# A two-layer decoder trunk on one core: the engines' order in the middle passes of the MLPs is written out slot by slot

## The chip, the cores and the metric

The kernel runs on one core of one Trainium2 chip. The time is the device time of one execution in microseconds (us). The engines of the core are called as the profile calls them: PE (TensorE, matrix products), PEld (its weight loads), DVE (VectorE), ACT (ScalarE), POOL (GpSimd) and SP (SyncE, which issues the loads here). Each engine works through its own list of instructions from front to back and waits where an input is not there yet.

## The reference: what is computed

Two layers over 256 positions with a width of 2048. The first layer mixes with a gated short convolution, the second with latent attention; behind each mixer stands the same MLP, with a hidden width of 8192:

```python
def sq_relu_mlp(x, w1, w2):
    return jnp.square(jax.nn.relu(x @ w1)) @ w2

h = layer_norm(ALPHA * h + mix, ...)
h = layer_norm(ALPHA * h + sq_relu_mlp(h, mlp_w1[layer], mlp_w2[layer]), ...)
```

All inputs and outputs are float32. The change lies in the two MLPs.

## The kernel before: tiles, stages and order

**Precision.** A float32 operand is split into two parts, hi and lo: hi is a rounding cast on ACT (`split`, line 139) and lo the remainder on DVE (line 140). A product is made of the large parts and the two mixed terms. Every weight that is loaded (tiles `raw`, 128x1024, 512 KB, from a pool of 7) passes through such a cast and such a subtraction into a pair hi, lo (a pool of 9).

**The MLP in passes.** The hidden width is cut into 8 passes q of 8 blocks m of 128 columns. For one block, `mm_run` (16 pairs of matmuls, lines 227 and 231) makes `x @ w1` into a PSUM bank called "unit". `whole` then empties the bank: ACT copies its right half (line 370), DVE adds it to the left half into a row tile `fp` or `fq` (line 371). Only when that is done may the next `mm_run` write the bank. Relu and square follow on ACT (line 768), or for the last block on DVE (line 764).

**The middle passes, 1 to 6, and the first half of pass 7 in the second MLP** multiply with `w2` by Strassen's scheme: seven products in place of eight. For this, `form` (lines 655 to 666) makes sums of two neighbouring blocks on DVE, `finish_pair` splits the row into `factors` (tiles h1a, h1c, h3a, h3c; a cast of 128x896 on ACT and a subtraction on DVE), and the weights are combined too. A weight item is a pair of loads r1, r2. `prepare` makes of it t = b12 - r1 (line 174), two half-wide sums (lines 178 and 181), and the splits of r1, t, r2 and of a half-wide tile t4. The tile t is a `raw` too.

**Slots.** `steps` yields the slots (q, m). A slot holds the `mm_run` of block (q, m) and, where there is one, one product item: `fast_products`, 21 matmuls (lines 312 to 314) into seven PSUM banks. The product items run `SHIFT` = 6 blocks behind: slots 0 to 5 of pass 1 have none, nor in the first MLP the last two of pass 7. A slot without a product is called lone here. In the second MLP two products stand alone behind pass 7. The weights stand in `stream` in the order of the slots: two w1 halves (singles), then the w2 pair.

**Two column halves.** Products 0 to 3 of a pass belong to one half of the output columns, 4 to 7 to the other. When product 3 has ended, the seven sums are moved out of PSUM (`put_back`, line 624, ACT) and those of the other half moved in (`resume`, line 718, ACT). In the text one such pair of copies is a move. Behind the last middle pass, `fold` (line 632) adds up the sums on DVE, eight additions for a half, drawn by `next(folds)`.

**What sets the order before.** The matmuls of `mm_run` and `fast_products` are pinned to program order. DVE's and ACT's instructions are not: a scheduler orders them by program order as priority and by when their inputs are due. The weights are made ahead by `take`: a look ahead of 6 or 7 steps, where a single is one step and a pair three. The seven moves stand together in the program, behind the product that ends a half. The row of block 2 is a tile of its own, `fq`, since two rows are open there; all other rows share one `fp`. In the second MLP `issue_after` holds back what follows the last `finish_pair`.

Of the kernel before, what the change touches and what calls it, by code (L numbers as in the profile page):

```python
# [10 lines left out]
F32 = mybir.dt.float32  # L11
F32R = mybir.dt.float32r
AF = mybir.ActivationFunctionType
ALU = mybir.AluOpType
# [23 lines left out]
SHIFT = 6  # L38
# [18 lines left out]
def trunk(ctx: ExitStack, tc: tile.TileContext, xT, vecs, lead, w_first, w_in, w_out, w_kv, w_q, w_uk, w_uv,  # L57
# [95 lines left out]
    def prepare(i):  # L153

        if len(stream[i]) == 1:
            raw = load_raw(i, stream[i][0])
# [13 lines left out]
        finished(r1, f"{i}_1")  # L170
        yield
        t = raws.tile([P, 1024], F32, tag="raw", name=f"raw{i}_t")
        two = "p (a c) -> p a c"
        nc.vector.tensor_tensor(t.rearrange(two, a=2), b12.unsqueeze(1).to_broadcast([P, 2, BW]),  # L174
                                r1.rearrange(two, a=2), ALU.subtract)
        finished(t, f"{i}_t")
        yield
        nc.vector.tensor_tensor(b12, b22, t[:, :BW], ALU.subtract)  # L178
        finished(r2, f"{i}_2")
        t4 = r1[:, :BW]  # L180
        nc.vector.tensor_tensor(t4, b21, b12, ALU.subtract)  # L181
# [7 lines left out]
    def size(i):  # L189

        return 1 if len(stream[i]) == 1 else 3

    begun = {}
# [31 lines left out]
    def high(ps, w, blk, x, first):  # L225

        return nc.tensor.matmul(ps, w[blk // 8][0][:, blk % 8, :], x, start=first, stop=False)  # L227

    def low(ps, w, blk, x, last):

        return nc.tensor.matmul(ps[:, :T], w[blk // 8][1][:, blk % 8, :], x[:, :T], start=False, stop=last)  # L231

    def mm_run(wps, x, k0, k1, nk, turned=None, pin=lambda ins: ins):

        for k, (w, ps) in [(k, u) for k in range(k0, k1) for u in wps]:
            if k == turned:
                pin(low(ps, w, k, x[k], False))
            pin(high(ps, w, k, x[k], k == 0))
            if k != turned:
                pin(low(ps, w, k, x[k], k == nk - 1))  # L240
# [68 lines left out]
    def dot(ps, w, x, first, last, onto=False, pin=lambda ins: ins):  # L309


        pin(nc.tensor.matmul(ps, x[0], w[0], start=first, stop=False, skip_group_check=onto))  # L312
        pin(nc.tensor.matmul(ps, x[0], w[1], start=False, stop=False, skip_group_check=onto))  # L313
        pin(nc.tensor.matmul(ps, x[1], w[0], start=False, stop=last, skip_group_check=onto))  # L314
# [45 lines left out]
    def fast_products(ps, x, j, fresh, ready, onto=()):  # L360

        b, = take(1, 6)
        a = {n: [x[j // 2][:, j % 2, o, i * P:(i + 1) * P] for o in range(2)] for i, n in enumerate(LEFT, 1)}
        for p, l, r in FACTORS:
            dot(ps[p], b[r], a[l], p in fresh, p in ready, onto=p in onto, pin=tc.keep_in_program_order)
# [224 lines left out]
    def mlp(idx, ln, blocks, fast, begin=None, extra=None, last=False):  # L590
# [64 lines left out]
        def form(u, v):  # L655

            a21, a11, a22, a12, s1, s3, s2, s4 = ((u if i < 4 else v)[:, i * P:(i + 1) * P] for i in range(8))
            nc.vector.tensor_tensor(s1, a21, a22, ALU.add)
            if u is v:
                two = u.rearrange("p (i c) -> p i c", c=P)  # L660
                nc.vector.tensor_tensor(two[:, 5:7, :], two[:, 0:5:4, :], a11.unsqueeze(1).to_broadcast([P, 2, P]),
                                        ALU.subtract)
            else:
                nc.vector.tensor_tensor(s2, s1, a11, ALU.subtract)
                nc.vector.tensor_tensor(s3, a21, a11, ALU.subtract)
            nc.vector.tensor_tensor(s4, a12, s2, ALU.subtract)

        def finish_pair(j, u):
            f = factors[j // 2][:, j % 2]
            if q in FAST or last:  # L670
                v = row() if u.shape[1] < 8 * P else u
                form(u, v)
                at = P if q in FAST else 0
                if u is not v:
                    split(f[:, 0, at:4 * P], f[:, 1, at:4 * P], u[:, at:])
                    at = 4 * P
                return split(f[:, 0, at:], f[:, 1, at:], v[:, at:])
            return split(f[:, 0, :2 * T], f[:, 1, :2 * T], u[:, :2 * T])

        def row():  # L680
            return fast.tile([P, 8 * P], F32, tag="fp", name="fp")
# [29 lines left out]
        def resume(p, g, at=None):  # L711
# [3 lines left out]
            if p in OWN and begun[g] == FAST[0]:  # L715
# [5 lines left out]
        begun = {0: FAST[0], 1: FAST[0]}  # L721
        rows = {}
        behind = ExitStack()

        def products_of(p, i, j, g):
# [3 lines left out]
            end = i == 0 or p == FAST[-1] and not last  # L729
            fast_products(ps, factors, j, set(fresh), order if j == NB - 1 and end else (), onto)  # L730
            fresh.clear()
            if j == NB - 1 and end:
                begun[g] = 0
                for o in order:
                    if p == NQ - 1:
                        if o in OWN:
                            put_back(o, g, ps[o])
                        continue
                    put_back(o, g, ps[o])
                    if i == 0:  # L740
                        resume(o, 1 - g)
            if p == FAST[-1] and j == NB - 1 and end:
                folds = chain(folds, fold(g))

        for q, m, pair in steps(last):
            lone = pair is None
            if q == NQ:
                products_of(*pair)
                if pair[2] == NB - 1:
                    behind.close()  # L750
                continue
            if q == FAST[0] and m == SHIFT:
                for o, _, _ in FACTORS:
                    resume(o, 1)
            w = take(2, 7)
            at = "6" if lone and (m - SHIFT) % 2 else "unit"
            un = psum("ps_u", bank[at])
            mm_run([(w, un)], xhl, 0, NC, NC, turned=TURNED if TURN(q, m) else None, pin=tc.keep_in_program_order)
            if m % 2 == 0:
                u = act.tile([P, 2 * T], F32, tag="ab", name="fq") if m == 2 and not lone else row()  # L760
            whole(un, u[:, (m % 2) * T:(m % 2 + 1) * T])
            late = m >= QC - 2
            if late and m % 2:
                nc.vector.scalar_tensor_tensor(u[:, T:2 * T], u[:, T:2 * T], 0.0, u[:, T:2 * T], ALU.max, ALU.mult)
            elif late or m % 2:
                for function in (AF.Relu, AF.Square):
                    at = u[:, :T] if late else u[:, :2 * T]
                    nc.scalar.activation(at, at, function)
            if late and q not in FAST and not last:
                f, at = factors[m // 4][:, 1], slice(m % 2 * T, (m % 2 + 1) * T)  # L770
                split(f[:, 0, at], f[:, 1, at], u[:, at])
            else:
                rows[m // 2] = u
            if m % 2 and (m > 3 or lone) and m // 2 in rows:
                made = finish_pair(m // 2, rows.pop(m // 2))
                if last and q == NQ - 1 and m == QC - 1:
# [454 lines left out]
```

## Time and profile before

| | |
|---|---|
| median of 3 runs | 2020.77 us (2018.97 to 2022.5) |
| the profiled execution | 2020.92 us |
| its span | 2019.1 us |
| middle passes, first MLP | 452 to 1008 us of the span |
| middle passes, second MLP | 1405 to 1983 us of the span |

A row of the timeline gives the start in the span, the duration, the engine, the line of the kernel, the operation, the tiles (out<-in), and in square brackets how long the engine had stood idle before it and for whom. Durations of neighbours overlap a little, so what one instruction costs its engine in a busy stretch is the distance between two starts. A row of the waits gives who waited for whom, with the total, the number of times and the longest. A row of the windows gives for a stretch of time the busy time of each engine with the number of instructions, then PE's granted clock (1.00 is full speed), the share of the DMA engines and GB/s.

### The profile page before, as it was taken

Reading aid. Unit: us, or ns where it says so; the run is one execution under the profiler, and the core shown is the slowest. Engines: PE = TensorE matmul, PEld = TensorE weight load, DVE = VectorE, ACT = ScalarE, POOL = GpSimd, SP = SyncE. Lnnn points to the kernel's source line nnn. Section 1 sums busy time; section 2 is a strip of 40 time slices with the busy share of each in tenths; the row PEclk is TensorE's granted clock in tenths of the full one; section 3 lists DMA queues with packets and bytes.
Section 4 is the critical chain, followed back from the end, with each engine's and each line's share of the span. In section 5 each row is a group of like instructions: output and inputs, shape, how many; then the busy total and the mean of one; then the engine's idle time right before and its main releaser. Section 6 shows DMA issues by size and latency. Waiting matters only on the chain.

```text
span 2019.1 us, 29666 instructions
## 1 busy us (share of the span) xinstructions
PE 1990.8 (99%) x11050; PEld 1731.3 (86%) x11050; DVE 1747.1 (87%) x2562; ACT 1289.2 (64%) x1927; POOL 5.6 (0%) x27
## 2 busy tenths in 40 slices
PE   9999999999999999999999999999999999999998
PEld 8888888988888888888889998898888888888885
DVE  8667677778899999999998988777889999999998
ACT  6444445586667767677756665557666776767763
POOL 0000000000000000000000000000000000000000
PEclk9999999999999999999999999999999999999999
DMA  9666666575556555666665544556455556555554
GB/s 343 213 188 188 188 189 189 186 234 153 174 200 202 198 201 187 207 206 201 235 223 160 180 132 140 183 191 185 147 187 208 188 189 208 200 205 190 198 176 158
DMA packets 107712, 390.00 MB, mean 193 GB/s; under 512 B 11952, under 2 KB 12720, under 8 KB 107056
## 3 DMA queue, kind: packets, MB, share of 16 engines
q1 hardware_dynamic: 106560, 383.79, 57.6%
q0 software_dynamic: 864, 4.19, 0.5%
q8 instruction: 86, 1.41, 0.3%
q14 instruction: 58, 0.48, 0.1%
q10 hardware_dynamic: 144, 0.13, 0.0%
HBM read 383.87 MB, written 4.19 MB: 192 GB/s over the span
## 4 chain that ended last, share of the span: by engine, by line
PE 80%; DVE 10%; ACT 6%; issue 3%; DMA 1%; DVEq 0%; ACTq 0%
PE ps_u L227 15%; PE ps_l L227 13%; PE ps_u L231 8%; PE ps_l L231 7%; PE ps L313 5%; PE ps L314 5%; PE ps L312 4%; DVE lo L140 4%; PE ps_d L313 2%; PE ps_d L314 2%; PE ps_d L312 2%; ACT hi L139 2%; ACT ps L718 2%; PE ps_w L261 2%; PE ps_w L260 2%
## 5 line engine op out<-in xcount | busy, mean ns | idle before, releaser
L140 DVE TENSOR_TENSOR lo<-raw,hi 128x1024 fp32r<-128x1024 f32 x710 | 856.2, 1220 | 163.8 <-ACT hi L139 94.7
L139 ACT CAST hi<-raw 128x1024 fp32r<-128x1024 f32 x710 | 732.2, 1055 | 201.8 <-PE ps_l L227 102.2
L227 PE MATMUL ps_u<-xhl,hi 128*128 128x512 f32 x1792 | 624.4, 395 | 17.3 <-DVE fq L371 12.9
L231 PE MATMUL ps_u<-xhl,lo 128*128 128x256 f32 x1792 | 486.2, 280 | 0.0
L227 PEld LDWEIGHTS ps_u<-xhl,hi 128*128 128x128 f32 x1792 | 329.8, 188 | 90.2 <-DVE fq L371 17.2
L231 PEld LDWEIGHTS ps_u<-xhl,lo 128*128 128x128 f32 x1792 | 338.9, 189 | 12.2
L227 PE MATMUL ps_l<-xhl_a,hi 128*128 128x512 f32 x704 | 244.1, 393 | 0.0
L231 PE MATMUL ps_l<-xhl_a,lo 128*128 128x256 f32 x704 | 195.4, 279 | 0.0
L139 ACT CAST hi_t<-raw_t 128x1024 fp32r<-128x1024 f32 x100 | 105.9, 1059 | 118.3 <-DVE raw_t L174 111.2
L227 PEld LDWEIGHTS ps_l<-xhl_a,hi 128*128 128x128 f32 x704 | 132.1, 188 | 29.9
L370 ACT COPY t<-ps_u 128x256 f32<-128x256 f32 x112 | 41.9, 374 | 151.0 <-PE ps_u L231 151.0
L231 PEld LDWEIGHTS ps_l<-xhl_a,lo 128*128 128x128 f32 x704 | 131.9, 188 | 0.2
L174 DVE TENSOR_TENSOR raw_t<-raw,raw 128x1024 f32<-128x1024 f32 x100 | 121.9, 1219 | 6.6 <-DMA raw<-in_w2f_dram 6.6
L140 DVE TENSOR_TENSOR lo_t<-raw_t,hi_t 128x1024 fp32r<-128x1024 f32 x100 | 121.9, 1219 | 2.3 <-ACT hi_t L139 2.3
L227 PE MATMUL ps_l<-z,hi 128*128 128x512 f32 x240 | 82.4, 391 | 0.0
L261 PE MATMUL ps_w<-xd,hi 128*128 128x258 f32 x256 | 72.7, 284 | 0.0
L259 PE MATMUL ps_w<-xd,hi 128*128 128x258 f32 x256 | 72.3, 282 | 0.0
L260 PE MATMUL ps_w<-xd,lo 128*128 128x258 f32 x256 | 72.2, 282 | 0.0
L139 ACT CAST t<-raw 128x512 fp32r<-128x512 f32 x100 | 61.9, 619 | 15.4 <-DVE raw L181 15.2
L227 PE MATMUL ps_l<-oT,hi 128*128 128x512 f32 x208 | 71.3, 391 | 0.0
L181 DVE TENSOR_TENSOR raw<-raw 128x512 f32<-128x512 f32 x100 | 69.0, 690 | 2.3
L178 DVE TENSOR_TENSOR raw<-raw,raw_t 128x512 f32<-128x512 f32 x100 | 68.5, 685 | 1.0
(371 smaller groups left out, 3897.3 us busy)
## 6 DMA issues: line engine op xcount, KB each, us to landing
raw<-in_w_dram SPq DMA_DIRECT2D x312, 512.0 KB, 4.2
raw<-in_w2f_dram SPq DMA_DIRECT2D x200, 512.0 KB, 5.1
raw<-in_w_in_dram SPq DMA_DIRECT2D x88, 512.0 KB, 3.7
raw<-in_w_out_dram SPq DMA_DIRECT2D x32, 512.0 KB, 3.7
raw<-in_w_o_dram SPq DMA_DIRECT2D x32, 512.0 KB, 4.2
raw<-in_w_kv_dram SPq DMA_DIRECT2D x10, 512.0 KB, 4.5
raw<-in_w_q_dram SPq DMA_DIRECT2D x8, 512.0 KB, 3.9
raw<-in_w_uk_dram SPq DMA_DIRECT2D x8, 512.0 KB, 4.4
```

The costliest lines, as they stand in the source:

```text
L139: nc.scalar.copy(hi, src)
L140: return nc.vector.tensor_tensor(lo, src, hi.bitcast(F32), ALU.subtract)
L174: nc.vector.tensor_tensor(t.rearrange(two, a=2), b12.unsqueeze(1).to_broadcast([P, 2, BW]), r1.rearrange(two, a=2), ALU.subtract)
L181: nc.vector.tensor_tensor(t4, b21, b12, ALU.subtract)
L227: return nc.tensor.matmul(ps, w[blk // 8][0][:, blk % 8, :], x, start=first, stop=False)
L231: return nc.tensor.matmul(ps[:, :T], w[blk // 8][1][:, blk % 8, :], x[:, :T], start=False, stop=last)
L259: nc.tensor.matmul(ps[:, :W], hi, x[k][:, :W], start=k == 0, stop=False)
L260: nc.tensor.matmul(ps[:, :W], lo, x[k][:, :W], start=False, stop=False)
L261: nc.tensor.matmul(ps[:, :W], hi, x[k][:, W:], start=False, stop=k == NC - 1)
L312: pin(nc.tensor.matmul(ps, x[0], w[0], start=first, stop=False, skip_group_check=onto))
L313: pin(nc.tensor.matmul(ps, x[0], w[1], start=False, stop=False, skip_group_check=onto))
L314: pin(nc.tensor.matmul(ps, x[1], w[0], start=False, stop=last, skip_group_check=onto))
```

## The change

The lists of PE, DVE and ACT in the middle passes become the program's own order: a class `Order` links each instruction of these three engines to the one before it on the same engine. SP is not linked. `SHIFT` becomes 5: the lone slots are slots 0 to 4 of pass 1 and, in the first MLP, the last three of pass 7; one product stands alone at the end of the second MLP. What a slot needs is made wholly in the slot in front of it. `prepare` has five steps for a pair in place of three, and they are laid between the slot's other work; the moves are taken one at a time from a list and laid between the splits. A slot that begins with open moves is called crowded in the code. With `SHIFT` 5 only one row is open at a time, so `fq` goes, and each row is formed and split in one piece. The number of matmuls is the same. The remaining edits (`pin`, `two`, names) only follow from this.

```diff
-SHIFT = 6
+SHIFT = 5
...
     def prepare(i):
...
+            raw = loaded.pop(i) if i in loaded else load_raw(i, stream[i][0])
...
         r1, r2 = (load_raw(f"{i}_{j}", src) for j, src in enumerate(stream[i]))
+        t = raws.tile([P, 1024], F32, tag="raw", name=f"raw{i}_t")
...
-        finished(r1, f"{i}_1")
-        yield
...
         nc.vector.tensor_tensor(t.rearrange(two, a=2), b12.unsqueeze(1).to_broadcast([P, 2, BW]),
                                 r1.rearrange(two, a=2), ALU.subtract)
+        yield
+        finished(r1, f"{i}_1")
+        yield
+        nc.vector.tensor_tensor(b12, b22, t[:, :BW], ALU.subtract)
+        t4 = r1[:, :BW]
+        nc.vector.tensor_tensor(t4, b21, b12, ALU.subtract)
         finished(t, f"{i}_t")
         yield
-        nc.vector.tensor_tensor(b12, b22, t[:, :BW], ALU.subtract)
         finished(r2, f"{i}_2")
-        t4 = r1[:, :BW]
-        nc.vector.tensor_tensor(t4, b21, b12, ALU.subtract)
+        yield
         f = state["fast"].tile([P, 2, BW], F32R, tag="t4", name=f"t4_{i}", bufs=2)
         split(f[:, 0, :], f[:, 1, :], t4)
...
+    class Order:
+        def __init__(self):
+            self.at, self.last = len(tc.nc.cur_bb.bb.instructions), {}
+        def keep(self):
+            traced = tc.nc.cur_bb.bb.instructions
+            for i in traced[self.at:]:
+                if i.engine in ENGINES:
+                    if i.engine in self.last:
+                        tc.add_manual_dep(i, self.last[i.engine], mybir.DependencyInfo(
+                            mybir.DependencyClass.NoSync, mybir.DependencyReason.DATA), reason="order")
+                    self.last[i.engine] = i.name
+            self.at = len(traced)
...
+        def move(n):
+            for _ in range(n):
+                if moves:
+                    o, g, on = moves.pop(0)
+                    put_back(o, g, ps[o])
+                    if on:
+                        resume(o, 1 - g)
...
+        order = Order()
+        for s, (q, m, pair, own) in enumerate(slots):
             lone = pair is None
...
+            following = slots[s + 1][3] if s + 1 < len(slots) else []
+            pairs = [i for i in following if size(i) > 1]
+            ahead = [i for i in range(state["next"], (following or own)[-1] + 1) if i not in own and i not in begun]
+            if not pairs:
+                ahead = [i for i in range(state["next"], own[-1] + 6) if i not in own and i not in begun]
+                ahead = ahead[:next((k for k, i in enumerate(ahead) if size(i) > 1), len(ahead))]
+            singles = [i for i in ahead if size(i) == 1]
+            for i in singles:
+                loaded[i] = load_raw(i, stream[i][0])
...
+            if q < NQ:
+                w = take(2, 0)
+                at = "6" if lone and (m - SHIFT) % 2 else "unit"
+                un = psum("ps_u", bank[at])
+                mm_run([(w, un)], xhl, 0, NC, NC, turned=TURNED if TURN(q, m) else None)
...
+            crowded = len(moves) > 0
+            for i in pairs:
+                step(i)
+            for i in singles:
+                step(i)
+                move(1)
+            if crowded:
+                evacuate()
+            for i in pairs:
+                step(i)
+            move(len(moves))
+            for i in pairs:
+                step(i)
+            if rows and m == 2:
+                finish_pair(0, rows.pop(0))
             if pair:
                 products_of(*pair)
-            if m in (2, 3) and not lone:
-                finish_pair(m - 2, rows.pop(m - 2))
+            if not crowded:
+                evacuate()
+            if q < NQ and m == QC - 1:
+                forms(rows[m // 2])
+            move(1)
+            for i in pairs:
+                step(i)
+            move(1)
+            if q < NQ and m == QC - 1:
+                finish_pair(m // 2, rows.pop(m // 2))
+            for i in pairs:
+                step(i)
+            move(2)
+            if q < NQ:
+                if m % 2 or m == QC - 2:
+                    u = rows.get(m // 2)
+                    if m < QC - 1:
+                        at = u[:, :T] if m == QC - 2 else u[:, :2 * T]
+                        for function in (AF.Relu, AF.Square):
+                            nc.scalar.activation(at, at, function)
+                        if m % 2:
+                            forms(u)
+                            if m > 1 or lone:
+                                finish_pair(m // 2, rows.pop(m // 2))
...
+                if q == NQ - 1 and m:
+                    for _ in range(3 if m >= SHIFT else 2):
+                        next(folds, None)
+            order.keep()
+        move(len(moves))
```

Here `evacuate` is `whole` (with line 764 for block 7), and `step(i)` makes the next step of item i.

More of the change, by code (lines that the diff above doesn't have):

```diff
@@ L742, in products_of @@
-            if p == FAST[-1] and j == NB - 1 and end:
-                folds = chain(folds, fold(g))
-        for q, m, pair in steps(last):
-            lone = pair is None
[L747 to L751, printed above, removed]
+            if end:
+                opened[g] = 0
+                moves.extend((o, g, i == 0 and p < NQ - 1) for o in order if p < NQ - 1 or o in OWN)
+                if p == FAST[-1]:
+                    folds = chain(folds, fold(g))
@@ L752, in mlp @@
             if q == FAST[0] and m == SHIFT:
+                sums = act.tile([P, 4, 2, BW], F32, tag="xres", name=f"sums{idx}")
                 for o, _, _ in FACTORS:
                     resume(o, 1)
[L755 to L773, printed above, removed]
```

120 lines of the change are left out of this document (54 added, 66 removed).

## The prediction

> **What bounds the kernel now.** I read the busy shares first, then what PE waited for, then one steady pass of the middle passes in the windows and what DVE waited for in it (the last two rows), then the timeline around PE's wait.
>
> ```profile
> span 2019.1 us, 29666 instructions
> PE 1990.8 (99%) x11050; PEld 1731.3 (86%) x11050; DVE 1747.1 (87%) x2562; ACT 1289.2 (64%) x1927; POOL 5.6 (0%) x27
> ...
> PE ps_u L227 <- DVE fq L371: 12.9, 10, 1.8
> PE ps_u L227 <- DVE fp L371: 4.4, 4, 1.6
> PE ps L313 <- DVE lo_t L140: 1.0, 1, 1.0
> PE ps L312 <- ACT hi_t L139: 0.6, 1, 0.6
> ...
> 709.70:794.27 84.57, 83.21 (x425) 70.59 (x425) 80.12 (x100) 60.16 (x84) 0.00 (x0) 1.00 0.60 199
> ...
> DVE lo L140 <- ACT hi L139: 3.6, 2, 3.4
> DVE fp L371 <- ACT t L370: 0.5, 1, 0.5
> ```
>
> PE is the busiest, and nothing here makes its work smaller: the most that an order can win is its waits. But the steady pass is not PE's. DVE is busy 80.12 of its 84.57 us and waits 4.1 for ACT (the last two rows); the 0.35 left are small gaps. So DVE closes the loop, and PE waits once a pass, for the bank that DVE empties late. The reason stands in the timeline:
>
> ```profile
> 697.88 0.58 ACT L624 COPY acc<-ps 128x512 f32<-128x512 f32 x1
> 698.35 0.59 ACT L624 COPY sums<-ps 128x512 f32<-128x512 f32 x1
> 698.83 0.60 ACT L718 COPY ps<-acc 128x512 f32<-128x512 f32 x1
> 699.35 0.60 ACT L718 COPY ps<-sums 128x512 f32<-128x512 f32 x1
> ...
> 705.28 0.64 ACT L718 COPY ps<-acc 128x512 f32<-128x512 f32 x1
> ...
> 705.47 1.23 DVE L140 TENSOR_TENSOR lo<-raw,hi 128x1024 fp32r<-128x1024 f32 x1 [3.70 <-ACT hi L139]
> ...
> 709.70 0.50 PE L227 MATMUL ps_u<-xhl,hi 128*128 128x512 f32 x1 [1.37 <-DVE fq L371]
> ```
>
> ACT makes the seven moves nearly in one go, from 697.88 to 705.9; no cast comes out, DVE stands still for 3.70, and 4 us later PE waits 1.37 for DVE. A move costs ACT 0.47 + 0.52 = 1.0 by the starts.
>
> **The lengths.** What an instruction costs a busy engine is the distance of two starts:
>
> ```profile
> 680.50 2.35 DVE L140 TENSOR_TENSOR lo<-raw,hi 128x1024 fp32r<-128x1024 f32 x2
> 682.77 1.22 DVE L174 TENSOR_TENSOR raw_t<-raw,raw 128x1024 f32<-128x1024 f32 x1
> 683.91 0.42 DVE L371 TENSOR_TENSOR fp<-ps_u,t 128x256 f32<-128x256 f32 x1
> 684.24 0.68 DVE L178 TENSOR_TENSOR raw<-raw,raw_t 128x512 f32<-128x512 f32 x1
> 684.96 0.69 DVE L181 TENSOR_TENSOR raw<-raw 128x512 f32<-128x512 f32 x1
> 685.57 1.22 DVE L140 TENSOR_TENSOR lo_t<-raw_t,hi_t 128x1024 fp32r<-128x1024 f32 x1
> ...
> 1971.38 0.29 DVE L658 TENSOR_TENSOR fp<-fp 128x128 f32<-128x128 f32 x1
> 1971.70 0.42 DVE L661 TENSOR_TENSOR fp<-fp 128x256 f32<-128x256 f32 x1
> 1972.16 0.29 DVE L666 TENSOR_TENSOR fp<-fp 128x128 f32<-128x128 f32 x1
> 1973.57 1.23 DVE L140 TENSOR_TENSOR h3a<-fp,h3a 128x1024 fp32r<-128x1024 f32 x1 [1.12 <-ACT h3a L139]
> ...
> 651.53 0.39 PE L312 MATMUL ps<-hi,h1a 128*128 128x512 f32 x1
> ...
> 656.34 0.39 PE L227 MATMUL ps_u<-xhl,hi 128*128 128x512 f32 x1
> ...
> 661.90 0.39 PE L312 MATMUL ps<-hi,h1c 128*128 128x512 f32 x1
> ```
>
> A full-wide DVE instruction costs 1.135, emptying the bank 0.33 (its end 0.42 behind its start), the half-wide ones 0.72 (the next one needs it) and 0.61; t4's split, half-wide too, 0.60. Two groups of ACT in the steady pass and one of the whole run give the casts of a row, relu and square, and the copy of the bank:
>
> ```profile
> L139 ACT CAST h1a<-fp 128x896 fp32r<-128x896 f32 x2 | 1.9, 947 | 0.0
> L768 ACT ACTIVATE fp<-fp 128x512 f32<-128x512 f32 x4 | 2.5, 628 | 0.0
> ...
> L370 ACT COPY t<-ps_u 128x256 f32<-128x256 f32 x112 | 41.9, 374 | 151.0 <-PE ps_u L231 151.0
> ```
>
> On PE a product takes 4.81 (651.53 to 656.34) and an `mm_run` 5.56, so a slot 10.37 and eight 82.96.
>
> **The change, on DVE.** Per slot six full-wide instructions, t4's sums and split and the emptying: 6.81 + 0.72 + 0.61 + 0.60 + 0.33 = 9.07, before as after. The order decides what else is lost. Before the emptying now stand t, both singles, r1, the half-wide sums and the split of t: 7.0 us, then 0.42. If DVE begins a slot's list by a lag L behind PE, PE waits as soon as L + 7.42 exceeds 10.37, that is at L over 2.95. The slots then differ:
> - Blocks 4, 6 and 0: only the 9.07. L falls by 1.30.
> - Blocks 3 and 5: the forms stand together, so each waits for the one before (0.32 + 0.46); then ACT must cast the row before DVE may subtract, and nothing stands between. The last rows above show just this: 1.41 from the last form to the subtraction; the cast of 128x896 is some 0.10 shorter than that of 128x1024, so 1.31; the subtraction 1.00 (1.09 less the overlap). Together 3.09; L grows by 1.79. Now other splits lie in these gaps.
> - Block 7: line 764, 0.45, forms 0.98, and the subtraction 1.00 (r2's split covers the cast): L grows by 1.13.
> - Block 1: forms 0.98, and the moves. Four of them lie in slot 0, behind the product; with r2's cast, which waits for DVE's sum, ACT is through about 2.0 us into slot 1. DVE comes at lag 1.4 and then waits: for the first single 0.6, for the second behind a move 0.8, for ACT's copy of the bank 0.1, for r1's cast 0.6. That is 2.1, where the bunch cost 4.1. L grows by 1.78.
> - Block 2: row 0 is subtracted ahead of the emptying, 1.00: L falls by 0.30, but 8.0 + 0.42 stand before the bank is free.
>
> The sum of a pass is 8 x 9.07 + 2 x 3.09 + 2.43 + 3.08 + 1.0 = **85.25 us, against 84.57 now**: the bunch's wait is halved, but waits for the row's cast (2.2 in blocks 3 and 5) and in the forms come instead. PE has to wait 85.25 - 82.96 = 2.3 a pass. In place: L is 3.2 behind block 1, so block 2's bank is free at 3.2 + 8.42 = 11.6, 1.3 late; behind blocks 3 and 5 L is about 3.4, and blocks 4 and 6 are 0.4 late each; 0.1 is lost at each restart.
>
> **Where passes begin.** In a lone slot DVE has little to do, but its list waits for PE, and behind the bank of block 3 stands a chain: ACT's copy 0.37, DVE's add 0.42, relu and square of 0.63 each, forms 1.1, cast 0.95, subtraction 1.0, some 5.4 with the hand-overs. Only then begin the parts of the first pair, 6.8 us of DVE in a slot of 5.56 of PE. L comes to 6.7 in slot 5, whose bank is free at 6.7 + 7.42 = 14.1: 3.7 late, and 1.7 more in the next, 5.5 in all. From below: the start now loses 1.6 in one wait at a bank (the longest of the four fp waits). I take the middle, 3.5.
>
> **Where they end.** Eight `fold` additions of 0.60 lie in blocks 1 to 4 of pass 7, 4.8 us. In the first MLP the last three slots are lone and swallow most of it: 2.8 of waits. In the second DVE's surplus of that pass is 2.3 + 4.8; PE waits 6.9.
>
> ```profile
> L632 DVE TENSOR_TENSOR acc<-acc,sums x18: 678/686/694, 956.2 to 1938.5; 128x512 f32<-128x512 f32 x18
> ...
> 963.83 0.50 PE L227 MATMUL ps_u<-xhl,hi 128*128 128x512 f32 x1 [1.81 <-DVE fq L371]
> ...
> 965.00:970.50 5.50, 5.50 (x24) 4.76 (x23) 5.50 (x7) 1.65 (x3) 0.00 (x0) 0.69 0.52 187
> ...
> 1918.10 0.50 PE L227 MATMUL ps_u<-xhl,hi 128*128 128x512 f32 x1 [1.81 <-DVE fq L371]
> ...
> 1922.00:1926.00 4.00, 4.00 (x22) 3.41 (x21) 4.00 (x5) 0.37 (x1) 0.00 (x0) 1.00 0.76 278
> ...
> 1978.00:1984.00 6.00, 5.42 (x17) 4.33 (x18) 6.00 (x7) 5.79 (x9) 0.00 (x0) 0.72 0.73 188
> ```
>
> **The clock.** Behind the wait of 1.81 at 963.83 PE ran below full clock: a mean of 0.69 over 5.5 us, 1.7 us lost. Behind the same wait at 1918.10 it did not. Behind the two waits of the first fence's last rows, near 1978, it did: 6 x 0.28, another 1.7. Of two waits of 1.8, one costs it; the new order has four of that size (two starts, two in the last pass), so I count two drops, 3.4, between none and 6.8. The Trainium skill ("TensorE: Matmul & The Clock Gate", part 1, what is actually happening) has the clock halve after an idle window of about 3.4 us; the 1.81 contradicts it as a threshold on one wait. By it alone only the two starts could pay, 3.4 again at the upper bound of their length and nothing at the lower, which would make the sum 3.4 less.
>
> **The rest.** Matmuls: the same number, `TURN` on one block more in pass 1 and one less in pass 7. Without `fq` a row costs DVE one form and one subtraction less, about 0.15 a pass, in the sum already. Loads: each takes the `raw` buffer of a tile two slots older; r2's is free when the second single is split, at L + 3.5, and lands 5.1 later, at L + 8.6, before the next slot's t at about L + 10.4. Hidden with 1.8 to spare.
>
> ```profile
> raw<-in_w2f_dram SPq DMA_DIRECT2D x200, 512.0 KB, 5.1
> ```
>
> **The sum.** Lost now: 17.3 + 1.6 in the waits of the first rows, 14 x 0.25 at restarts (a wait of 1.37 lengthens the slot by 1.62, 84.57 - 82.96), 3.4 by the clock: 25.8. Lost after: ten steady passes (2 to 6 in each MLP) x 2.3 = 23.0; starts 2 x 3.5 = 7.0; ends 2.8 + 6.9 = 9.7; clock 3.4: 43.1. The profiled execution took 2020.92, within 0.2 of the median of the runs, so 2020.9 + 17.3 = **2038 us**.
>
> **The rivals.**
> - *The spread moves free DVE, and PE becomes the bound.* Mechanism: in slots 0 and 1 of a pass ACT stays ahead, and rows are cast without a wait. It decides once DVE's waits and gaps fall so far that the pass's 85.25 comes under 82.96, so by 2.3 of the 4.3 us of waits. Then only the starts (3.5 to 7) remain of 25.8: about 2000. For it: ACT is busy 60.16 of 84.57. Against it: the cast behind the forms has no cover in blocks 3 and 5. Chance 0.10.
> - *Half of it.* DVE's 2.1 in slot 1 vanish (ACT gets through slot 0 a little sooner), the casts' 2.2 stay: a pass of 83.15, PE waits 0.2. Ten passes 2, starts 7, ends 9.7 - 4 = 6, one drop 1.7: 16.7 against 25.8, 2012. Chance 0.14.
> - *It comes out even*, with starts at their lower bound, one drop or none, and a pass at 84.6; or the scheduler's old order was nearly this one, so that the change changes little. The second is unlikely: DVE's 4.1 us of waits now hold none for the cast of a row, and the new list has one in blocks 3 and 5. 2017 to 2025. Chance 0.12.
> - *Loads come late.* If r2 landed 6.9 us or more behind its issue, not 5.1, DVE's first instruction would wait, and each further us would cost up to 1 us in each of 99 slots with a product. At 0.5 us: 2038 + 50 = 2088. Against it: the median. Chance 0.04.
>
> **How the numbers follow.** Forecast 0.60: 2027 to 2048 (starts at 1.6 and no drop take 7 off; starts at 5.5 and all four drops add 7; 0.3 us a pass either way 3). Faster by over 0.2% (4 us, about what can be told from no change): 0.10 + 0.14 = 0.24. Same: 0.12. Slower: 0.60 + 0.04 = 0.64. The range leaves out most of the first rival and the late loads: 2010 to 2048.
>
> **What would show it.** Right: in a steady pass DVE still closes the loop, with PE's waits for fp at the starts of blocks 3, 5 and 7, the largest at 3; DVE waits for ACT's h cast of about 1 us in blocks 3 and 5, and for hi in slot 1; a wait of several us in pass 1 for the bank. Wrong: a steady pass of 83 us; DVE waiting for PE (it is ahead); waits for DMA in front of raw_t.

## The result and the profile after

| | before | after |
|---|---|---|
| median, us | 2019.91 (4 runs beside the new ones) | 2050.47 (2049.0 to 2052.51, 4 runs) |
| ratio, 95% interval | 1 | 1.015 (1.0132 to 1.0167) |
| span of the profiled execution, us | 2019.1 | 2047.2 |

The kernel became 1.5% slower: 30.6 us by the medians, 28.1 by the spans. Cut at PE's first and last instruction of the middle passes, the spans differ by 12.3 us in the first MLP's middle passes (555.2 to 567.5), 18.6 in the second's (578.7 to 597.3), 1.9 between the two MLPs and -4.2 behind the last.

In the new numbering ACT's copy of the bank is line 399 and DVE's add line 400; the moves are lines 653 and 738, the forms 688 to 691, t line 172, the half-wide sums 177 and 179, `mm_run` lines 255 and 259, and the casts and subtractions still 139 and 140. First the page of the kernel after, its head:

```profile
span 2047.2 us, 29648 instructions
...
PE 2000.4 (98%) x11050; PEld 1733.2 (85%) x11050; DVE 1757.3 (86%) x2539; ACT 1308.1 (64%) x1915; POOL 5.7 (0%) x27
```

What PE waited for in it (total, times, longest), the largest rows:

```profile
PE ps_u L255 <- DVE fp L400: 38.3, 32, 4.1
PE mu0p L454 <- DVE xback L452: 1.6, 1, 1.6
```

Before, the wait for a bank was 17.3 us in 14 waits; now it is 38.3 in 32. The matmuls are the same in number and PE's own slots are still 10.37. So 21.0 of the 28.1 us are the wait that was there before, more often and longer. PE's busy time grows by 9.6 as well; the clock drops that lie in it are looked at below. The steady pass, as a row of the windows of the kernel after, and what DVE waited for in the same stretch:

```profile
787.40:873.90 86.50, 84.39 (x424) 71.51 (x423) 81.14 (x98) 61.58 (x83) 0.00 (x0) 0.98 0.59 195
```

```profile
DVE lo L140 <- ACT hi L139: 2.3, 3, 0.9
DVE h1a L140 <- ACT h1a L139: 1.1, 1, 1.1
DVE h1c L140 <- ACT h1c L139: 1.1, 1, 1.1
DVE fp L400 <- ACT t L399: 0.2, 1, 0.2
```

A pass takes about 86.5 us, 3.54 above PE's own 82.96 (before: 84.57). DVE is busy 81.14 and waits 4.7 for ACT: it is still the engine that closes the loop. Where it waits stands in its timeline, kernel after:

```profile
733.18 0.28 DVE L688 TENSOR_TENSOR fp<-fp 128x128 f32<-128x128 f32 x1
...
735.32 1.09 DVE L140 TENSOR_TENSOR h1c<-fp,h1c 128x896 fp32r<-128x896 f32 x1 [1.07 <-ACT h1c L139]
736.33 1.22 DVE L172 TENSOR_TENSOR raw_t<-raw,raw 128x1024 f32<-128x1024 f32 x1
...
789.61 1.23 DVE L140 TENSOR_TENSOR lo<-raw,hi 128x1024 fp32r<-128x1024 f32 x1 [0.94 <-ACT hi L139]
791.70 1.23 DVE L140 TENSOR_TENSOR lo<-raw,hi 128x1024 fp32r<-128x1024 f32 x1 [0.86 <-ACT hi L139]
793.10 0.43 DVE L400 TENSOR_TENSOR fp<-ps_u,t 128x256 f32<-128x256 f32 x1 [0.18 <-ACT t L399]
794.05 1.23 DVE L140 TENSOR_TENSOR lo<-raw,hi 128x1024 fp32r<-128x1024 f32 x1 [0.53 <-ACT hi L139]
```

From the first form of block 3 to the next weight tile's t pass 3.15 us (733.18 to 736.33), 1.07 of them waiting for the row's cast. In block 1 DVE waits four times, 2.51 together, behind ACT's moves. PE pays for it two slots later, and most where the middle passes begin. PE's timeline of the kernel after, at the two starts (494 and 1464), at three starts of a block 3, and at block 3 of the last pass (1953):

```profile
494.15 0.50 PE L255 MATMUL ps_u<-xhl,hi 128*128 128x512 f32 x1 [3.71 <-DVE fp L400]
...
722.51 0.50 PE L255 MATMUL ps_u<-xhl,hi 128*128 128x512 f32 x1 [2.22 <-DVE fp L400]
...
809.06 0.50 PE L255 MATMUL ps_u<-xhl,hi 128*128 128x512 f32 x1 [2.11 <-DVE fp L400]
...
1464.50 0.50 PE L255 MATMUL ps_u<-xhl,hi 128*128 128x512 f32 x1 [4.08 <-DVE fp L400]
...
1692.84 0.50 PE L255 MATMUL ps_u<-xhl,hi 128*128 128x512 f32 x1 [2.18 <-DVE fp L400]
...
1953.81 0.80 PE L255 MATMUL ps_u<-xhl,hi 128*128 128x512 f32 x1 [3.53 <-DVE fp L400]
```

At all of these but the one at 722.51 the clock falls, in the wait or right behind it. Windows of the kernel after, PE's granted clock third from the end:

```profile
495.60:499.01 3.41, 3.41 (x13) 2.92 (x12) 2.27 (x6) 2.10 (x3) 0.00 (x0) 0.50 0.81 257
809.60:813.01 3.41, 3.41 (x12) 2.84 (x11) 3.41 (x5) 1.46 (x2) 0.00 (x0) 0.51 0.55 143
1465.00:1468.41 3.41, 3.41 (x13) 2.93 (x12) 2.28 (x6) 1.90 (x4) 0.00 (x0) 0.50 0.49 127
1693.70:1697.11 3.41, 3.41 (x12) 2.92 (x12) 3.41 (x5) 1.19 (x2) 0.00 (x0) 0.50 0.60 169
1953.10:1959.92 6.82, 6.11 (x19) 5.24 (x20) 6.72 (x9) 2.62 (x3) 0.00 (x0) 0.50 0.48 156
```

Six stretches of 3.41 us at half clock, the last two adjacent in the last pass, each half a stretch of lost work for PE. Before, the middle passes held two. What they add to the time is another question, answered by an experiment below.

### The profile page after: what moved, and what is told of

Its sections match the earlier page's. It is cut to its first block, busy times and chain, and to the rows that moved or that the text cites. A ratio compares the mean times of both kernels' runs of the same rounds, so it can differ in the third digit from the quotient of the medians.

```text
span 2047.2 us, 29648 instructions
## 1 busy us (share of the span) xinstructions
PE 2000.4 (98%) x11050; PEld 1733.2 (85%) x11050; DVE 1757.3 (86%) x2539; ACT 1308.1 (64%) x1915; POOL 5.7 (0%) x27
## 4 chain that ended last, share of the span: by engine, by line
PE 54%; DVE 33%; ACT 7%; issue 5%; DMA 1%; DVEq 0%; ACTq 0%
DVE lo L140 15%; PE ps_l L255 13%; PE ps_l L259 7%; PE ps_u L255 5%; DVE lo_t L140 4%; DVE raw_t L172 3%; PE ps_u L259 3%; ACT hi L139 3%; DVE raw L177 2%; DVE raw L179 2%; DVE t L140 2%; PE ps_d L342 2%; PE ps_d L343 2%; PE ps_d L340 2%; PE ps_w L289 2%
## 5 line engine op out<-in xcount | busy, mean ns | idle before, releaser
L255 PE MATMUL ps_u<-xhl,hi 128*128 128x512 f32 x1792 | 634.5, 400 | 38.3 <-DVE fp L400 38.3
L842 ACT ACTIVATE fp<-fp 128x512 f32<-128x512 f32 (+1 forms) x112 | 64.9, 580 | 26.5 <-DVE fp L400 24.7
L400 DVE TENSOR_TENSOR fp<-ps_u,t 128x256 f32<-128x256 f32 x112 | 47.0, 420 | 35.7 <-ACT t L399 34.4
```

Of the source, the lines that this page charges most:

```text
L400: nc.vector.tensor_tensor(out, ps[:, :T], t, ALU.add)
```

## The experiments

All start from the kernel after unless it says otherwise, and all compute the whole result. Ratios are against the kernel before, run on the same chip, with 95% intervals. The medians of before lie between 2018.2 and 2020.9 us from one set of runs to the next, so a difference between medians of two sets is good to some 3 us; where it matters, the length of the middle passes (both MLPs together) in the two profiled executions stands beside it. The theory: DVE closes the loop, and the written order makes it wait at three places, each of which can be mended alone. Its rivals: the order is not to blame but `SHIFT` 5, the steps or the smaller horizon of loads; or only one of the two linked lists is.

### Three places, mended one by one

**The moves.** Each `resume` stands directly behind its own `put_back` and needs its result. ACT's timeline in the kernel after:

```profile
784.60 0.57 ACT L653 COPY sums<-ps 128x512 f32<-128x512 f32 x1
785.21 0.59 ACT L738 COPY ps<-sums 128x512 f32<-128x512 f32 x1
785.73 0.62 ACT L139 CAST t<-raw 128x512 fp32r<-128x512 f32 x1
```

From the copy out to the copy in pass 0.61, from there to the next instruction 0.52: a move is 1.13, not 1.0. The edit puts the previous bank's `resume` behind the next bank's `put_back`:

```diff
-        moves = []
+        moves, waiting = [], []
...
                     put_back(o, g, ps[o])
+                    if waiting:
+                        resume(*waiting.pop())
                     if on:
-                        resume(o, 1 - g)
+                        waiting.append((o, 1 - g))
+                    if waiting and not moves:
+                        resume(*waiting.pop())
```

> Changed kernel with one edit: a resume no longer stands right behind the put_back of the same bank, but behind the next bank's put_back. Theory A (waits that the written order itself puts on DVE: behind the moves, behind the cast of a row, at the start): a move falls from 1.13 to 1.0 us of ACT, DVE leaves block 1 some 0.75 earlier, PE's wait at the start of block 3 falls from 2.3 to about 1.4, twelve times: about -9 us, 2041. Rival B (any fixed order of DVE and ACT loses against the scheduler's, no single place matters): within 3 us of 2050. Rival C (SHIFT 5 leaves rows too little time): no change.

2042.96 us (2042.25 to 2046.19), ratio 1.0121 (1.0104 to 1.0138): 7.5 won by the medians, 5.9 in the middle passes. ACT's timeline of this kernel has the distance back at 0.48 and 0.52:

```profile
784.86 0.58 ACT L653 COPY sums<-ps 128x512 f32<-128x512 f32 x1
785.34 0.60 ACT L738 COPY ps<-sums 128x512 f32<-128x512 f32 x1
785.86 0.59 ACT L653 COPY sums<-ps 128x512 f32<-128x512 f32 x1
```

The slot in which PE meets the late bank, block 2's, shrinks from 12.74 to 12.06, and a pass from 86.5 to 85.9.

**The row's cast.** The split of a row made in blocks 3 and 5 is put behind the next slot's t:

```diff
-        rows = {}
+        rows, owed = {}, []
...
             for i in pairs:
                 step(i)
+            while owed:
+                j = owed.pop()
+                finish_pair(j, rows.pop(j))
...
-                            if m > 1 or lone:
+                            if m > 1 and pairs:
+                                owed.append(m // 2)
+                            elif m > 1 or lone:
                                 finish_pair(m // 2, rows.pop(m // 2))
```

> Changed kernel with one edit: in blocks 3 and 5 the cast and subtraction of the row stand behind the next slot's first step (t) and no longer at the end of their own slot. Theory A: DVE's waits of 1.1 for the cast go in both blocks, PE's waits at blocks 5 and 7 go, the one at block 3 falls a little because DVE comes to the moves less late: -1.4 us a pass, about -19 in all with the starts and ends, 2032. Rival B: within 3 us of 2050. Rival C (rows too late): slower, since two rows are ready later still.

2034.16 us (2032.6 to 2037.64), ratio 1.0077 (1.0058 to 1.0095): 16.3 won by the medians, 17.6 in the middle passes, the largest of the three. DVE's timeline of this kernel shows the cast covered by t, without a wait:

```profile
730.62 0.29 DVE L691 TENSOR_TENSOR fp<-fp 128x128 f32<-128x128 f32 x1
730.83 1.22 DVE L172 TENSOR_TENSOR raw_t<-raw,raw 128x1024 f32<-128x1024 f32 x1
731.98 1.09 DVE L140 TENSOR_TENSOR h1c<-fp,h1c 128x896 fp32r<-128x896 f32 x1
```

PE's waits at the starts of blocks 5 and 7 are gone (those slots are 10.37 again), and the one at block 3 is 1.75. A pass takes 84.96.

**The starts.** The first pair's parts are begun one slot earlier, in the lone slot of block 3:

```diff
+            if not pairs and q == FAST[0] and s + 2 < len(slots):
+                pairs = [i for i in slots[s + 2][3] if size(i) > 1]
```

> Changed kernel with one edit: the parts of the first pair of each MLP are made in the lone slot 3 of pass 1, not in slot 4. Theory A: PE's two waits in pass 1 (slots 5 and 6, 5.8 us together in each MLP) fall to about 0.9, nothing else moves: about -9.5 us, 2041. Rival B and C: within 3 us of 2050.

2043.77 us (2042.66 to 2045.36), ratio 1.0122 (1.0106 to 1.0139): 6.7 won by the medians, 4.9 in the middle passes, less than expected. Slot 5 falls from 14.29 to 10.71 in the first MLP, and from 14.6 to 12.6 in the second. Slot 6 stays at 12.22 in both, and here it can be seen what a clock drop costs. Its two ends in the second MLP and PE's clock in between, first in this kernel, from the timeline and the windows:

```profile
1458.54 0.50 PE L255 MATMUL ps_u<-xhl,hi 128*128 128x512 f32 x1 [2.08 <-DVE fp L400]
...
1470.76 0.50 PE L255 MATMUL ps_u<-xhl,hi 128*128 128x512 f32 x1 [1.59 <-DVE fp L400]
```

```profile
1459.00:1469.00 10.00, 10.00 (x53) 8.34 (x51) 8.83 (x12) 6.25 (x9) 0.00 (x0) 1.00 0.53 172
```

Full clock, and at the end a wait of 1.59: 12.22 us. In the kernel after the same slot begins at 1464.50 (above), has the window at 0.50, and ends without a wait:

```profile
1476.72 0.50 PE L255 MATMUL ps_u<-xhl,hi 128*128 128x512 f32 x1
```

12.22 us again. DVE sets the length of the slot; a PE at half clock only uses up the time that it would have waited. That holds for one stretch: in the run with the moves apart two stretches lie side by side in this slot of the second MLP (1459.6 to 1466.4 at 0.50), and it takes 13.01.

**All three together**, the engines still linked:

> Changed kernel, all three engines linked, with the three edits together: resume apart from its put_back, the row's cast covered in blocks 3 and 5, the first pair's parts in slot 3. Theory A (the waits at three places are the whole cost of the written order): the savings add, -7.5 - 16.3 - 6.7 = -30.5, and some more as block 3's wait shrinks further: 2015 to 2020, as fast as before. Rival B (a written order loses at many places): not under 2030.

2016.56 us (2015.16 to 2019.78, 10 runs), ratio 0.9988 (0.9978 to 0.9997). The gains add up (7.5 + 16.3 + 6.7 = 30.5, measured 33.9; in the middle passes 28.3 and 32.8), and the steady pass is 84.5 with one wait left, at block 3. So what the three places cost is as much as the whole difference between the two kernels. That does not make them all that the written order costs: the kernel with the three edits is only as fast as before, although it has the shorter `SHIFT` and the spread moves. The next runs ask what these are worth without the links.

### Without the links

**Only PE is linked**; DVE and ACT are ordered by the scheduler again, everything else is the changed program:

```diff
-    ENGINES = (mybir.EngineType.PE, mybir.EngineType.DVE, mybir.EngineType.Activation)
+    ENGINES = (mybir.EngineType.PE,)
```

> Changed kernel with one edit: only PE's instructions are linked in order; DVE's and ACT's are left to the scheduler, with SHIFT 5, the five steps and one-slot horizon as they are. Rival B: back to about 2020. Theory A: the scheduler may fill the waits behind the row's cast and the moves, but the horizon and the program's sequence stay: between 2025 and 2045. Rival C: stays at 2050.

**1998.79 us (1997.35 to 1999.55), ratio 0.9897 (0.9878 to 0.9916): faster than both kernels.** All three expectations missed it. A row of its windows:

```profile
705.10:788.00 82.90, 82.90 (x426) 70.63 (x425) 79.45 (x98) 60.85 (x83) 0.00 (x0) 1.00 0.60 203
```

PE is busy without a gap, at full clock. DVE is busy 79.45 with the same 98 instructions that took 81.14 in the written order. Its timeline shows how:

```profile
740.66 0.28 DVE L688 TENSOR_TENSOR fp<-fp 128x128 f32<-128x128 f32 x1
740.86 1.22 DVE L140 TENSOR_TENSOR lo<-raw,hi 128x1024 fp32r<-128x1024 f32 x1
741.99 0.42 DVE L689 TENSOR_TENSOR fp<-fp 128x256 f32<-128x256 f32 x1
742.33 1.22 DVE L140 TENSOR_TENSOR lo<-raw,hi 128x1024 fp32r<-128x1024 f32 x1
743.47 0.28 DVE L691 TENSOR_TENSOR fp<-fp 128x128 f32<-128x128 f32 x1
743.67 0.69 DVE L177 TENSOR_TENSOR raw<-raw,raw_t 128x512 f32<-128x512 f32 x1
744.27 1.22 DVE L140 TENSOR_TENSOR lo_t<-raw_t,hi_t 128x1024 fp32r<-128x1024 f32 x1
745.40 1.09 DVE L140 TENSOR_TENSOR h1a<-fp,h1a 128x896 fp32r<-128x896 f32 x1
```

In these rows no instruction stands directly behind the one that it needs. The three forms cost 0.20, 0.34 and 0.20 where a chain of them cost 0.32, 0.46 and 0.2; the first half-wide sum costs 0.60, not 0.72; and the row's cast on ACT lies under 745.40 - 743.67 = 1.73 us of other work. Of the 3.60 us that a pass is shorter than after, 1.69 are busy time and 1.9 waits of DVE.

**The bunch again.** In that kernel, all seven moves behind the product, as before the change:

```diff
             if pair:
                 products_of(*pair)
+                move(len(moves))
```

> Kernel with only PE linked (1998.8), with all seven moves again in one go in the program, right behind the product that ends a half; the scheduler still orders DVE and ACT. If the spread moves are what gains beside SHIFT 5: DVE waits for casts behind the bunch, PE waits 1 to 1.5 in one block of each pass as in the kernel before with SHIFT 5, about 2011. If the scheduler lays the moves anyhow and the five steps with the one-slot horizon gain: within 3 us of 1999.

2007.03 us (2005.71 to 2007.82), ratio 0.9933 (0.9918 to 0.9948): 8.2 slower than with the moves spread (10.7 in the middle passes), nearer to the first expectation. PE's waits in this kernel have one large row, which is 0.6 in one wait with the moves spread:

```profile
PE ps_u L255 <- DVE fp L400: 8.5, 8, 2.0
```

**The kernel before with `SHIFT` 5**, nothing else:

> Kernel before with SHIFT 5 and nothing else. With the changed kernel unpinned on DVE and ACT at 1998.8, something else in the change gains. If it is SHIFT 5: about 2000. If it is the spread moves, the five steps or the one-slot horizon: within 4 us of before, 2018. If SHIFT 5 leaves rows too little time: slower than 2022.

2011.95 us (2010.97 to 2015.31, 7 runs), ratio 0.9965 (0.9953 to 0.9977): 7.6 won, between the first two expectations. DVE's instructions are as many as before (2562), so it is the distance alone. But little of it is won where it was looked for: in the profiled execution (2014.88, above the median) the middle passes are only 0.5 us shorter than before, and 5.7 are won behind them. There a wait of PE for ACT is 1.6 in place of 4.1, and the stretch at half clock that the kernel before has at 2009.5 is missing. In the first MLP pass 4 is PE's own 82.93, passes 5 and 6 still lose 1.2 each, and in pass 2 of both the rows come late:

```profile
PE ps L314 <- DVE h3a L140: 5.0, 3, 3.7
```

One slot there loses 4.1 in the first MLP and 6.6 in the second. Waits explain 1.9 and 3.7 of it; most of the rest is PE at half clock (0.50 from 520.9 to 524.2 and from 1473.2 to 1479.9). No wait follows there in which the loss could hide. The changed program with only PE linked, whose row is split in one piece, loses 1.05 and 1.4 in those slots.

**Only one of the two lists linked.** First PE and ACT, DVE free; then PE and DVE, ACT free:

```diff
+    ENGINES = (mybir.EngineType.PE, mybir.EngineType.Activation)
...
+    ENGINES = (mybir.EngineType.PE, mybir.EngineType.DVE)
```

> Changed kernel with PE's and ACT's lists linked and DVE left to the scheduler. If DVE's list is what costs (the subtraction of a row stands directly behind its forms): DVE fills the 1.1 us in blocks 3 and 5 and the start, about 2020; the wait behind the moves in block 1 stays, since ACT's list sets it. If ACT's list is what costs: about 2045.

> Changed kernel with PE's and DVE's lists linked and ACT left to the scheduler. DVE still waits 1.1 for the row's cast in blocks 3 and 5 and still makes the first pair late; only the moves may be laid better: about 2040. If ACT's list is what costs: about 2010.

2035.68 us (2034.16 to 2036.63), ratio 1.008 (1.0064 to 1.0096), and 2066.54 us (2064.39 to 2067.05), ratio 1.0232 (1.0215 to 1.0248). The first lies between its two expectations: the waits at blocks 5 and 7 are gone, and the one at block 3 stays, now 2.5. The second is worse than either, and worse than with both linked. With DVE linked and ACT free, ACT's waits between 690 and 1000 us are led by:

```profile
ACT hi_t L139 <- DVE raw_t L172: 36.7, 18, 3.0
ACT hi L139 <- DVE raw L177: 30.6, 20, 2.6
```

ACT's own order asks for tiles that DVE's list makes later. So neither list is to blame alone: against the free program, ACT's list costs 37 us, DVE's 68 and both together 52. That the scheduler's half and the written half do not fit each other is what these waits suggest; it was not tested further. Whether some written pair of lists could reach 1998.8 was not tried beyond the three edits.

### A lighter DVE

If DVE closes the loop, taking t4's subtraction (0.60 a slot) from it should help the linked kernel. POOL takes it:

```diff
-        split(f[:, 0, :], f[:, 1, :], t4)
+        nc.scalar.copy(f[:, 0, :], t4)
+        nc.gpsimd.tensor_tensor(f[:, 1, :], t4, f[:, 0, :].bitcast(F32), ALU.subtract)
```

> Changed kernel, all three linked, with t4's subtraction on POOL in place of DVE: 0.60 us less of DVE in every slot with a product, 4.8 a pass. Theory A (DVE's list closes the loop): PE's waits at blocks 5 and 7 go and the one at block 3 falls from 2.3 to about 1.5, starts and ends lose less: about 2028. If DVE is not the bound but ACT's and PE's places in the lists are: within 5 us of 2050. If POOL's work slows DVE's: DVE's full-wide instruction grows over 1.22 us and the gain is smaller or none.

2093.27 us (2090.98 to 2096.41), ratio 1.0357 (1.034 to 1.0374): 42.8 slower than after. The timelines of this kernel on POOL and on DVE:

```profile
707.83 1.73 POOL L186 TENSOR_TENSOR t<-raw,t 128x512 fp32r<-128x512 f32 x1 [7.92 <-ACT t L185]
719.06 1.32 POOL L186 TENSOR_TENSOR t<-raw,t 128x512 fp32r<-128x512 f32 x1 [9.50 <-ACT t L185]
```

```profile
708.32 2.32 DVE L172 TENSOR_TENSOR raw_t<-raw,raw 128x1024 f32<-128x1024 f32 x1
...
719.13 2.33 DVE L140 TENSOR_TENSOR lo<-raw,hi 128x1024 fp32r<-128x1024 f32 x1
```

DVE's instruction takes 2.32 instead of 1.22, and both times it ends 1.08 us behind the end of POOL's (709.56 and 720.38). So it goes through the whole run: 99 of POOL's 100 subtractions overlap a DVE instruction that is held up, by 87 us in sum, where 60 were saved, and DVE's busy time grows by 30, from 1757.3 to 1787.4. DVE's add of the bank (line 401 here), which reads one of its inputs from PSUM, is not held up: 0.42 beside POOL as ever, 42 times. The other 13 of the 42.8 us were not told apart. A part may lie in PE's clock, whose mean is 0.982 and not 0.995: in the first MLP the passes with two stretches at half clock side by side take 91.5 and 90.9, and those with one 89.8 and 89.7. The same edit in the kernel with only PE linked:

> The kernel with only PE linked, with t4's subtraction on POOL. Its steady passes are at PE's own 82.93 already, so DVE's relief can only take the waits left in the first passes and the ends, some 9 us at most: 1990 to 1999.

2102.43 us (2098.09 to 2104.31), ratio 1.0403 (1.0387 to 1.0418), a miss as well, 103.6 slower than without the edit. Here DVE's busy time hardly changes (1738.3, without the edit 1737.7), so the loss is another one: the scheduler has laid the list anew. ACT makes the moves close together again, from 707.0 to 716.3 in one pass, and DVE waits for a cast:

```profile
713.41 1.23 DVE L140 TENSOR_TENSOR lo<-raw,hi 128x1024 fp32r<-128x1024 f32 x1 [5.20 <-ACT hi L139]
```

Why it did so stays open. This pair of runs tells nothing of a lighter DVE; the first shows what POOL costs it.

## Why the prediction was right in kind and too small

**Right.** DVE closes the loop of a steady pass, and the waits came where they were put: PE at the starts of blocks 3, 5 and 7, the largest at 3; DVE for the row's cast in blocks 3 and 5 and for hi in block 1; several us at the bank in pass 1. Sizes that held: the row in block 3, forecast 3.09, measured 3.15; PE's waits at blocks 5 and 7, forecast 0.4, measured 0.2 to 0.3 (with the restart the slots in front are 0.4 to 0.45 over 10.37); loads hidden. The three edits that remove one of these causes each won 7.5, 16.3 and 6.7 us, so they are causes and not only neighbours.

**Too small**, by these terms of the sum. PE's losses by their place; measured is a stretch's length less its slots' own:

| us | forecast | measured |
|---|---|---|
| ten steady passes | 23.0 | 863.6 - 829.6 = 34.0 |
| two starts (pass 1) | 7.0 | 5.9 + 6.3 = 12.2 |
| two ends | 9.7 | 2.3 + 9.1 = 11.4 |
| clock, as a term of its own | 3.4 | in the rows above |
| sum | 43.1 | 57.6 |

The sum grew by 14.5. Counted the same way, the kernel before lost 26.8 and not 25.8, and 2.7 come back outside the middle passes (-4.2 behind them against 1.9 and -0.4), for which the prediction had no term: PE's wait of 4.1 there is 1.6 now, and the stretch at half clock at 2009.5 is gone. So the profiled execution came out at 2049.0, 11 over the forecast of 2038. The ends were 2.3 and 9.1, forecast 2.8 and 6.9; why the second is longer was not traced.

- *"A move costs ACT 0.47 + 0.52 = 1.0 by the starts."* The starts were those of a bunch in which no copy waits for the copy in front of it. In the new order each does: 0.61 + 0.52. DVE shows what it does to a pass, by the distance from one t to the next: block 1 takes 12.94 us (700.90 to 713.84) where 9.07 + 3.08 = 12.15 was forecast, and 12.32 with the moves apart. All blocks of that pass take 86.55 where 85.25 was forecast, so this step is about half of the miss in a steady pass, 0.62 of 1.30. The rest is spread: 0.17 more in block 1, 0.20 in block 2, 0.18 in block 7, 0.12 in blocks 3 and 5 together. In part it is the same mistake on DVE: in block 7, line 804 stands directly behind the emptying that it needs, and the two starts are 0.45 apart, not 0.33; and behind a wait an instruction costs its whole 1.22, not 1.135. The row to ask was there: the prediction priced DVE's forms higher because each waits for the one before, and did not ask the same of ACT's copies.
- *"I take the middle, 3.5."* The working of the upper bound, 3.7 late in slot 5 and 1.7 in the next, was nearly exact: slot 5 is 3.9 and 4.2 over, slot 6 is 1.85. The lower bound, 1.6, was the start of the old order, in which DVE was free to run ahead, and says nothing of a list that has to wait. The middle was chosen where one bound had a mechanism and the other only a neighbour.
- *"So I count two drops, 3.4."* There were six, but the error is of another kind: a drop is no term of its own where DVE sets the time. At the starts it takes the place of a wait, as the two slots of 12.22 show. In a steady pass too: behind the drop at 809.6 the next slots are 12.06, 10.37, 10.37 and 10.37, where a pass without one has 10.48, 10.8, 10.5 and 10.8; together with a shorter block 2 in the next pass (12.32, not 12.7) nearly all of its 1.7 is back. In the last pass the kernel after has two stretches and the one with the early pair has one; its slots of blocks 2 to 4 are 14.06, 13.25 and 10.69 in the first and 14.01, 12.05 and 11.89 in the second, the same in sum. The Trainium skill's threshold ("TensorE: Matmul & The Clock Gate", part 1, what's actually happening), an idle window of about 3.4 us, fits the starts' 3.71 and 4.08; the drops behind 2.11 and 2.18 contradict it as a threshold on one wait, as the 1.81 did before.
- *"Of two waits of 1.8, one costs it"*. The traces show what tells them apart. The stretches begin on a fixed grid: 495.62 and 809.64 are 92 times 3.413 us apart, and so on through every trace. What counts is how much of one window of this grid PE stands idle. The wait of 1.81 before 963.83 lies in one window, as do the 2.11 and the 2.18; the one before 1918.10 is cut at 1917.36 into 1.07 and 0.74, and the 2.22 before 722.51 at 720.89 into 0.60 and 1.62. From 450 us on, the thirteen traces have 55 windows at full clock with 1.88 us or more of such idle time, and half clock follows each; it follows 5 of the 33 between 1.6 and 1.88, and none of those with less. The grid lies differently in each execution, so which of two such waits pays is luck, and no count of drops could have been forecast from the lengths.

**What the prediction did not see** is how much the rest of the change is worth. It put what goes with `fq` at 0.15 a pass and gave the first rival, spread moves that free DVE until PE is the bound at about 2000 us, a chance of 0.10, because the row's cast had no cover in blocks 3 and 5. The rival's price is met (1998.8) as soon as DVE and ACT are not held to the written order, and PE is then the bound; its objection names one of the things that the links put back. But its mechanism, the spread moves, carries only a part of the gain, so that the price fits so well is in part luck. From before to the fastest kernel and on to after:

| | median, us | middle passes of the profiled execution, us |
|---|---|---|
| before | 2019.91 | 1134.3 |
| `SHIFT` 5 alone | 2011.95 | 1133.8 |
| the changed program, only PE linked, moves in one go | 2007.03 | 1127.7 |
| the same, moves spread | 1998.79 | 1117.0 |
| DVE and ACT linked too: after | 2050.47 | 1165.1 |
| after with the three edits | 2016.56 | 1132.3 |

The links cost 52 us, and the three edits win 34 of them back; where the other 18 lie was not traced. The third row holds several edits that were not told apart: the five steps, the row in one piece, the order of the loads, the draws of the folds and the end of `issue_after`.

## What to carry to other kernels

Where one engine is busy some 95% of a loop, each instruction that stands directly behind the one it needs, on the same engine or through another, is time that the loop cannot give back; lay something independent between them before the order is fixed, and price dependent neighbours by a dependent row of the trace. A change that restructures work and also fixes its order should be run with the order left free as well: here the same program was 1% faster than before when free and 1.5% slower when fixed. Two engines that hand tiles to each other need lists written as a pair, since fixing one of them alone can cost more than fixing both.

## What the hardware showed beside this

A subtraction on POOL with inputs in SBUF holds up a DVE subtraction of two SBUF tiles wholly: 2.32 us instead of 1.22, ending 1.08 behind POOL's end. The Trainium skill ("SBUF — State Buffer") says that a DVE instruction with two SBUF inputs contends with a GpSimd instruction that reads SBUF (who interferes with whom), and that whichever starts first holds the shared ports for the whole instruction while the other fully blocks (SBUF: two separate sides); the trace agrees.

PE's clock falls to half for 3.41 us when PE has stood idle for more than some 1.9 us of one window of a fixed grid of 3.413 us: 55 of 55 windows with 1.88 us or more, 5 of 33 between 1.6 and 1.88, none with less. So a wait of 1.81 can cost a stretch where one of 2.22, cut by the grid, does not.

One such stretch costs a loop that another engine closes almost nothing: the slot of 12.22 us is as long with a window at 0.50 as with a wait of 1.59 at full clock. Two side by side can cost (13.01 in that slot), and where no wait follows, as in pass 2 of the kernel before with `SHIFT` 5, it costs PE the half of its time.
